# Other queues for q and gates, later weight requests, and values stored by row group in a layer of neighbourhood attention and retention

## The chip, the cores and the metric

The kernel runs on one core of one Trainium2 chip. Five engines work side by side, each with its own instruction queue: TensorE (PE; its weight loads are listed as PEld), VectorE (DVE), ScalarE (ACT), GpSimd (POOL) and SyncE (SP), which only issues DMAs. ScalarE issues DMAs too, between its computing instructions. A DMA that must wait (for a free buffer, or for data that is not there yet) holds every later instruction of the engine that issues it. The metric is the device time of one execution in microseconds (us), lower is better.

## What is computed

One layer for 2048 latent tokens (a grid of 32 rows by 64 columns) and 256 context tokens, width 1024, all in float32:

```python
h_lat = _rmsnorm(x, norm_g[i]) * (1.0 + scale) + shift          # adaLN from SiLU(c)
na_q, na_k, na_v, na_g, r_q, r_k, r_v, r_g = _split_proj(h_lat @ w_in)     # 8 parts of 512 columns
...
# group A: 8 heads of 64; each query reads an 8 x 16 window of the grid and all 256 context keys
s_loc = jnp.einsum('bhrqd,bhrkd->bhrqk', qr, kg, ...) * scale + bias[None]
p = jax.nn.softmax(jnp.concatenate([s_loc, s_ctx], axis=-1), axis=-1)
o = jnp.einsum('bhrqk,bhrkd->bhrqd', p_loc, vg) + jnp.einsum('bhrqc,bhcd->bhrqd', p_ctx, v_ctx)
y_na = _merge(o_na) * jax.nn.silu(na_g)
# group B: 4 heads of 128, retention in both directions, chunks of 128 tokens
y_ret = _head_rmsnorm(o_ret, ret_norm_g).astype(dt) * jax.nn.silu(r_g)
y_lat = jnp.concatenate([y_na, y_ret], axis=-1) @ w_out
x = x + gate * y_lat                                            # then one final RMSNorm
```

## The kernel before

The kernel keeps float32 accuracy by splitting an operand into a high and a low part (names `whi`, `wlo`, `hhi`, `hlo`) and adding three products. Results of the projection go to HBM (tensors `qS`, `kS`, `vS`, `gS` for group A; `rqS`, `rkS`, `rvS`, `ggS` for group B) and come back when they are needed. The stages, in time of the profiled execution:

- 0 to 156 us: norm, modulation and the k projection.
- 156 to 556 us: the first part of the projection: values of group A (`u_v`, 18 units of 256 tokens, two of them context, 166 to 280 us), gates, q of group A. Stores are issued by ScalarE here.
- 556 to 1082 us: neighbourhood attention, 128 tiles of 128 queries (8 rows by 16 columns): per head `h` four windows `i` of 8 rows, in each four tiles `j` of 16 columns. A tile's scores (`s_mm`) use the k tile of its head, `k2` (128 partitions: the high half of 64 dimensions on top of the low half) and the window's q tile, `q` (the same 64 rows in both halves of the partitions, two buffers). Softmax runs over VectorE (`s_min`), ScalarE (`s_exp`) and GpSimd (`s_norm`), transposes (`p_tr`) and the product with the values (`pv`) follow two and three tiles later. Values come as tiles `vt` of four grid rows, six buffers, with four slots by tile column: columns 0 to 23, 8 to 39, 24 to 55 and 40 to 63 (the table `CWIN`).
- Between the parts of a tile, `fill` runs steps of the rest of the projection (`fill_stream`: units of 8 steps for group B, four units to a weight block of 256 columns). It splits the next weights into high and low in pieces (`chop`), and `late_load` requests the block after.
- 1082 to 1430 us: retention and output projection.

All loads of the attention stage are on SyncE's queue, in the order in which the loop over tiles (at the end of `hybrid_kernel`'s attention part) calls them: `load_head` (k2 and the context values) once per head, at tile (1, 2) of the head before; `load_q` at the first tile of a window for the next window; `load_v` by group of four rows; `bias` for the three forms of position bias in a row of tiles; `load_gate` once per window; and, from `fill`, weights (`st`, line 173) and rotary tables (`rot`). A load of q is two DMAs of 64 rows, one for each half of the partitions; of k likewise; of a value group four, one for each tile column, each reading 4 grid rows of 24 or 32 positions.

Of the kernel before, what the change touches and what calls it, by code (L numbers as in the profile page):

```python
# [18 lines left out]
P = 128  # L19
# [55 lines left out]
        BN += _row[_c][0]  # L75
RTYPE = [0, 1, 1, 2]
CTYPE = [0, 1, 1, 2]


@with_exitstack  # L80
def hybrid_kernel(ctx: ExitStack, tc: tile.TileContext, a: dict, out: bass.AP):
# [3 lines left out]
    dram = ctx.enter_context(tc.tile_pool(name="dram", bufs=1, space=DRAM))  # L85
    qS = [dram.tile([4, P, 2, 512], F32, name=f"qS{t}") for t in range(4)]
    kS = [dram.tile([P, 2, LT], F32, name=f"kS{t}") for t in range(4)]
    vS = [dram.tile([LT, 4, P], F32, name=f"vS{t}") for t in range(2)]
    gS = [dram.tile([P, L], F32, name=f"gS{t}") for t in range(4)]
    rqS = [dram.tile([P, L], F32, name=f"rqS{r}") for r in range(RH)]  # L90
    rkS = [dram.tile([LT, 2 * P], F32, name=f"rkS{r}") for r in range(2)]
# [324 lines left out]
    def u_v(w, c0, tp):  # L416
        pm = yield from tokform(w, tp)
        vt = op.tile([P, 2, 2, 2, P], F32R, name="o")
        pv = pm.rearrange("p (t h e d) -> p t h e d", t=2, h=2, e=2)
        for e in range(2):  # L420
            hs, ls = slice(64 * e, 64 * e + 64), slice(64 - 64 * e, 128 - 64 * e)
            nc.scalar.copy(vt[:, :, :, e, hs], pv[:, :, :, e, :])
            nc.vector.tensor_tensor(vt[:, :, :, e, ls], pv[:, :, :, e, :], f(vt)[:, :, :, e, hs], ALU.subtract)
        store(vS[(c0 - 1024) // WG][tp * 256:(tp + 1) * 256].rearrange("(t p) h d -> p t (h d)", p=P),
              f(vt).rearrange("p t h e d -> p t (h e d)"))

    def put_tok(dstt, c0, tp, r, n=1):
        store(dstt[(c0 % 512) // WG][tp * 256:(tp + 1) * 256, :].rearrange("(t p) d -> p t d", p=P), r, n)
# [191 lines left out]
    def fill_stream(w):  # L620
        def units(kind, b):
            if kind is u_rq:
                return [(ct, b) for ct in range(2)]
            return [(2 * b + tp,) for tp in range(2)]

        def late_load(n):
            while chop:
                chop.pop(0)()
            if n == 0 and wseq:
                load_w()  # L630

        def next_c():
            w, parts = w_parts(*wcur.pop(0), n=4)
            chop.extend(parts)
            return w

        order = [(kind, *a_) for kind, c0 in fseq[:4] for b in range(2) for a_ in units(kind, b)]
        order += [(kind, *a_) for b in range(4) for kind, c0 in fseq[4:6] for a_ in units(kind, b)]
        order += [(kind, *a_) for kind, c0 in fseq[6:] for b in (2, 3) for a_ in units(kind, b)]
        at = [0]  # L640

        def needs(n):
            kind, *a_ = order[n] if n < len(order) else (None,)
            if kind is u_rk:
                return [("rot_k", a_[0])]
            if kind is u_rq and a_[0] == 0:
                return [("rot_c", a_[1]), ("rot_s", a_[1])]
            return []

        def steps(g):  # L650
            n = at[0]
            at[0] += 1
            is_rq = lambda k: k >= 0 and order[k][0] is u_rq
            if is_rq(n - 1):
                for e in needs(n)[1:]:
                    rot_load(*e)
            for m, v in enumerate(g):
                if m == 2:
                    for e in needs(n + 1)[:1 if is_rq(n) else 2]:
                        rot_load(*e)  # L660
                if chop:
                    chop.pop(0)()
                yield v

        for kind, c0 in fseq[:4]:
            wn = next_c()
            for n, args in enumerate(units(kind, 0) + units(kind, 1)):
                yield from steps(kind(w, c0, *args))
                late_load(n)
            w = wn  # L670
        (rk, ck), (rq, cq) = fseq[4:6]
        wn = next_c()
        for b in range(4):
            for n, args in enumerate(units(rk, b)):
                yield from steps(rk(w, ck, *args))
                late_load(n + b)
            if b == 3:
                w = next_c()
            for args in units(rq, b):
# [25 lines left out]

    def load_head(h):
        k2 = kp.tile([P, LT], F32R, name="k2")
        for hl in range(2):
            nc.sync.dma_start(f(k2)[64 * hl:64 * hl + 64, :], kS[h // 2][64 * (h % 2):64 * (h % 2) + 64, hl, :])
        vh = vS[h // 4][:, h % 4, :]  # L710
        vc = kp.tile([P, 2, P], F32R, name="vc")
        nc.sync.dma_start(f(vc), vh[L:, :].rearrange("(n p) d -> p n d", p=P))
        return dict(k2=k2, vh=vh, vc=vc, vt={}, q={})

    def load_q(hd, h, i):
        q = kp.tile([P, 2, 512], F32R, name="q", bufs=2)
        src = qS[h // 2][i, 64 * (h % 2):64 * (h % 2) + 64]
        for e in range(2):
            nc.sync.dma_start(f(q)[64 * e:64 * e + 64], src)
        hd["q"][i] = q  # L720

    def load_v(hd, gs):
        for g in gs:
            vt = kp.tile([P, 4, P], F32R, name="vt", bufs=6)
            src = hd["vh"][4 * g * GW:(4 * g + 4) * GW, :].rearrange("(r c) d -> r c d", c=GW)
            for j, (c0, cw) in enumerate(CWIN):
                nc.sync.dma_start(f(vt)[:4 * cw, j, :], src[:, c0:c0 + cw, :])
            hd["vt"][g] = vt

    def bias(h, rt, ct):  # L730
# [56 lines left out]
    def pv(t):  # L787
        h, i, j, kr0, kr, kc0, cw = dims(t)
        T, hd = tl_st[t], heads[h]
        pt, ng_ = T["pt"], T["ng"]  # L790
        if t % 2 == 0:
            tl_st["po"] = psc.tile([P, 2, 2, P], F32, name="po")
        po = tl_st["po"]
        cn = 4 * cw
        for g in range(ng_):
            nc.tensor.matmul(po[:, t % 2, :, :], hd["vt"][kr0 // 4 + g][:cn, j, :], pt[:cn, g, :, :], start=(g == 0), stop=False)  # L796
# [9 lines left out]
    def load_gate(t):  # L806
        h, i = dims(t)[:2]
        gts[t // 4] = ap_.tile([P, 512], F32, name="gt", bufs=2)
        nc.sync.dma_start(gts[t // 4][fin_(h)], gS[h // 2][fin_(h), i * 512:(i + 1) * 512])

    def combine(t):
        h, i, j = dims(t)[:3]
# [144 lines left out]
    for t in range(NT + 3):  # L957
        if t == 6:
            decay_exp(*dec)
        quota = (NF - held) * (t + 1) // (NT + 3) - done  # L960
        done += quota
        part = [quota // 3 + (quota % 3 > n) for n in range(3)]
        tick()
        if t < NT:
            s_mm(t)
        if 0 <= t - 1 < NT:
            s_norm(t - 1)
        fill(part[0])
        if t < NT:
            s_min(t)  # L970
        if 0 <= t - 2 < NT:
            p_tr(t - 2)
        if t < NT:
            s_exp(t)
        if 0 <= t - 2 < NT:
            p_lo(t - 2)
        fill(part[1])
        if 0 <= t - 3 < NT:
            pv(t - 3)
            if (t - 3) % 2 == 1:  # L980
# [12 lines left out]
        if i < 3 and j == 0:  # L993
            load_q(hd, h, i + 1)
        for g in {(0, 2): (3,), (0, 3): (4,), (1, 1): (5,), (1, 3): (6,), (2, 3): (7,)}.get((i, j), ()):
            load_v(hd, (g,))
        if h + 1 < NH:
            if i == 1 and j == 2:
                heads[h + 1] = load_head(h + 1)
            if i == 3:  # L1000
                nh = heads[h + 1]
                if j == 0:
                    load_q(nh, h + 1, 0)
                    bias(h + 1, 0, 0)
                    load_v(nh, (0,))
                if j == 2:
                    bias(h + 1, 0, 1)
                if j == 3:
                    bias(h + 1, 0, 2)
                    load_v(nh, (1, 2))  # L1010
    def load_y(lo, kind, t):
        half, o = t // 8, (t % 8) * P
        nc.sync.dma_start(f(lo), yS[half][4 * kind:4 * kind + 4, :, o:o + P].rearrange("k p t -> p k t"))
        return lo
# [331 lines left out]
```

## Time and profile before

| | us |
|---|---|
| median of 3 runs | 1429.25 (1426.46 to 1432.33) |
| the profiled execution, its own time | 1431.96 |
| its span, first to last instruction | 1430.0 |
| TensorE busy | 1351.1 (94%) |
| VectorE, ScalarE, GpSimd busy | 641.0, 531.0, 495.0 |
| mean granted clock of TensorE | 0.986 |
| moved by DMA | 264.14 MB, 185 GB/s over the span |

A row of windows gives a stretch of the span, each engine's busy time in it, the TensorE clock that was granted (1.00 is full), the mean busy share of the core's 16 DMA engines and the GB/s that they moved. A row of waits reads: who waited at which line, for whom, us in total, number of times, the longest. Rows of an instruction give its shortest, median and longest duration in ns; of a DMA that is the time of its issue, not of its transfer. SPq and ACTq are the queues on which SyncE and ScalarE issue.

### The profile page before, as it was taken

To read this page: it belongs to the slowest core of one execution; us is meant where nothing else is said; L and a number is where in the kernel's file an instruction comes from. 1 tells how busy PE (TensorE), PEld (TensorE's weight loads), DVE (VectorE), ACT (ScalarE), POOL (GpSimd) and SP (SyncE) were. 2 spreads that over 40 slices of the span, in tenths; PEclk is the share of its full clock that TensorE was granted. 3 is DMA by queue.
4 is the path that set the end of the run, shared out by engine and by line. 5 is a ranking of instruction groups with operands and counts; after the bars stand their busy time and mean duration, and the time that the engine had idled before them with its cause. 6 is when DMAs were issued, how large, how long until landed. Compare 5 with 4: busy or idle time off the path is not lost.

```text
span 1430.0 us, 22693 instructions
## 1 busy us (share of the span) xinstructions
PE 1351.1 (94%) x8380; PEld 1179.9 (83%) x8380; DVE 641.0 (45%) x1244; ACT 531.0 (37%) x1155; POOL 495.0 (35%) x499
## 2 busy tenths in 40 slices
PE   7989999999999999999899978798999989999997
PEld 2567899988887888998799877697999779888886
DVE  5786111100021222566666765476564544344445
ACT  5454212212212222655455433345563234333332
POOL 5442302202201221355354432235443144454442
PEclk9999999999999999999999998899999999999999
DMA  9444656223354677767758696867645998555433
GB/s 320 153 162 148 229 196 229 104 88 103 104 169 147 222 259 218 179 179 194 178 160 205 174 236 163 235 172 197 166 138 170 275 316 259 192 177 169 155 119 125
DMA packets 213072, 264.14 MB, mean 185 GB/s; under 512 B 14305, under 2 KB 160865, under 8 KB 211938
## 3 DMA queue, kind: packets, MB, share of 16 engines
q1 hardware_dynamic: 177282, 197.93, 48.1%
q10 hardware_dynamic: 35680, 64.76, 12.7%
q8 instruction: 67, 1.10, 0.3%
q14 instruction: 43, 0.35, 0.1%
HBM read 179.80 MB, written 82.84 MB: 184 GB/s over the span
## 4 chain that ended last, share of the span: by engine, by line
PE 73%; DMA 13%; DVE 7%; issue 2%; ACT 2%; POOL 2%; SPq 1%; ACTq 0%; DVEq 0%; POOLq 0%
PE mm L355 25%; PE mm L366 18%; PE mm L1190 10%; DMA q<-qS 5%; PE sS L748 4%; PE tr L775 2%; PE po L796 2%; DMA vt<-vS 2%; PE mm L915 2%; PE mm L299 2%; PE tr L777 1%; PE po L798 1%; DMA v<-rvS 1%; PE mm L1102 1%; PE mm L1101 1%
## 5 line engine op out<-in xcount | busy, mean ns | idle before, releaser
L355 PE MATMUL mm<-hhi,whi 128*128 128x512 f32 x640 | 260.0, 406 | 0.0
L355 PE MATMUL mm<-hlo,whi 128*128 128x512 f32 x640 | 254.0, 397 | 5.6 <-DVE hlo L268 2.2
L355 PE MATMUL mm<-hhi,wlo 128*128 128x512 f32 x640 | 253.8, 397 | 0.3 <-DVE wlo L336 0.3
L366 PE MATMUL mm<-whi,hhi 128*128 128x256 f32 x768 | 225.0, 293 | 0.0
L366 PE MATMUL mm<-wlo,hhi 128*128 128x256 f32 x768 | 217.3, 283 | 2.6 <-POOL wlo L336 2.6
L366 PE MATMUL mm<-whi,hlo 128*128 128x256 f32 x768 | 216.3, 282 | 0.0
L336 POOL TENSOR_TENSOR wlo<-st,whi 128x256 fp32r<-128x256 f32 (+1 forms) x97 | 112.3, 1175 | 251.1 <-ACT whi L334 250.8
L779 ACT CAST pt<-tr 128x640 fp32r<-128x640 f32 (+1 forms) x128 | 95.6, 747 | 217.9 <-PE tr L777 192.6
L785 DVE TENSOR_TENSOR pt<-tr,pt 128x640 fp32r<-128x640 f32 (+1 forms) x128 | 113.9, 890 | 105.2 <-ACT pt L779 104.6
L768 POOL TENSOR_SCALAR sp<-sp,stt 128x640 f32<-128x640 f32 (+2 forms) x128 | 103.7, 811 | 136.0 <-DVE stt L767 94.9
L366 PEld LDWEIGHTS mm<-wlo,hhi 128*128 128x128 f32 x768 | 145.4, 189 | 3.3 <-POOL wlo L336 3.2
L355 PEld LDWEIGHTS mm<-hlo,whi 128*128 128x128 f32 x640 | 121.0, 189 | 31.4 <-issue 3.2
L366 PEld LDWEIGHTS mm<-whi,hlo 128*128 128x128 f32 x768 | 145.7, 190 | 0.0
L366 PEld LDWEIGHTS mm<-whi,hhi 128*128 128x128 f32 x768 | 145.7, 190 | 0.0
L355 PEld LDWEIGHTS mm<-hhi,wlo 128*128 128x128 f32 x640 | 120.7, 189 | 29.5 <-DVE wlo L336 0.7
L355 PEld LDWEIGHTS mm<-hhi,whi 128*128 128x128 f32 x640 | 121.0, 189 | 28.5 <-issue 4.6
L757 DVE CUSTOM_DVE_ANT_0 sp<-sS,nb 128x640 f32<-128x640 f32 (+2 forms) x128 | 105.6, 825 | 53.4 <-PE sS L748 43.0
L748 PE MATMUL sS<-k,q 128*128 128x256 f32 (+3 forms) x512 | 101.7, 321 | 27.3 <-DMA q<-qS 21.8
L748 PEld LDWEIGHTS sS<-k,q 128*128 128x128 f32 x512 | 85.1, 192 | 36.5 <-issue 19.9
L762 ACT ACTIVATE sp<-sp,stt 128x640 f32<-128x640 f32 (+2 forms) x128 | 107.5, 839 | 20.1 <-DVE stt L757 19.8
L1190 PE MATMUL mm<-wor,y 128*128 128x512 f32 x384 | 95.6, 398 | 1.3 <-DVE xt L1199 1.2
L1190 PE MATMUL mm<-won,y 128*128 128x512 f32 x336 | 89.9, 406 | 0.0
(214 smaller groups left out, 2238.8 us busy)
## 6 DMA issues: line engine op xcount, KB each, us to landing
st<-in_w_in_dram SPq DMA_DIRECT2D x48, 512.0 KB
q<-qS SPq DMA_DIRECT2D x64, 256.0 KB
vS<-o ACTq DMA_DIRECT2D x18, 512.0 KB
k<-kS SPq DMA_DIRECT2D x16, 576.0 KB
kS<-o SPq DMA_DIRECT2D x16, 512.0 KB
woS<-g ACTq DMA_DIRECT2D x32, 256.0 KB
qS<-o ACTq DMA_DIRECT2D x16, 512.0 KB
vt<-vS SPq DMA_DIRECT2D x128, 64.0 KB
```

Of the source, the lines that this page charges most:

```text
L299: nc.tensor.matmul(aps[u][0:s.shape[2], :], s[:, 2 * j + k, :], w, start=(j == 0 and i == 0 and k == 0), stop=(j == 3 and i + 1 == len(ops ...
L336: eng.tensor_tensor(l, r, f(h), ALU.subtract)
L355: nc.tensor.matmul(pm[:, :n], ww[:, k, cs], h[:, k, :], start=(k == 0 and i == 0), stop=(k == KC - 1 and i == 2))
L366: nc.tensor.matmul(pm[:, t * WG:(t + 1) * WG], h[:, k, o:o + P], ww[:, k, :], start=(k == 0 and i == 0), stop=(k == KC - 1 and i == 2))
L748: nc.tensor.matmul(o, hd["q"][i][:, hl, j * P:(j + 1) * P], k, start=(hl == 0), stop=(hl == 1))
L757: nc.vector.tensor_tensor_reduce(T["sp"][:, :n], T["s"], nbz[big][:, o:o + n], -1.0, 3e38, ALU.add, ALU.min, T["st"][:, 0:1])
L762: nc.scalar.activation(sp[:, :n], sp[:, :n], AF.Exp, bias=st[:, 0:1], scale=-1.0, accum_out=st[:, 1:2])
L768: nc.gpsimd.tensor_scalar(sp[:, :n], sp[:, :n], st[:, 2:3], 0.0, ALU.mult, ALU.add)
L775: nc.tensor.transpose(tr[:cn, g, :], sp[:, T["lo"] + g * cn:T["lo"] + (g + 1) * cn], ident)
L779: nc.scalar.copy(pt[:, :ng_ + 2, 0, :], tr[:, :ng_ + 2, :])
L785: nc.vector.tensor_tensor(pt[:, :n, 1, :], tr[:, :n, :], f(pt)[:, :n, 0, :], ALU.subtract)
L1190: nc.tensor.matmul(pm, yy[:, k, :], ww[:, k, sl], start=(k == 0 and i == 0), stop=(k == 3 and i == 2))
```

## The change

Five things are edited.

1. `load_q` and `load_gate` are issued by ScalarE. `load_q` is one DMA instead of two: its source names the 64 rows twice, by a leading repeat of 2 with step 0.
2. `load_head` loads `k2` by one DMA whose source has the two halves as its leading dimension, then the 64 rows. It stays on SyncE's queue.
3. `late_load` requests the next weight block after the second unit of a block (`n == 1`), not after the first.
4. Latent values are stored in a new tensor `vB`, by group of four grid rows and tile column, in the form in which the attention reads them, so that columns that belong to two or three tile columns are stored that often. A unit of `u_v` issues eight stores (four tile columns, two row groups of 64 partitions) in place of one. `load_v` then loads a group by two DMAs, one of 128 partitions with two tile columns, one of 96 with the other two. Slots in a tile follow `VORD`.
5. Bias rows for the first window of the next head are loaded one tile later, the third of them at that head's first tile; so is the first value group of the next head.

```diff
+VORD = [1, 2, 0, 3]
...
-    vS = [dram.tile([LT, 4, P], F32, name=f"vS{t}") for t in range(2)]
+    vS = [dram.tile([LC, 4, P], F32, name=f"vS{t}") for t in range(2)]
+    vB = [dram.tile([P, 8, 4, 4 * P], F32, name=f"vB{t}") for t in range(2)]
...
-        store(vS[(c0 - 1024) // WG][tp * 256:(tp + 1) * 256].rearrange("(t p) h d -> p t (h d)", p=P),
-              f(vt).rearrange("p t h e d -> p t (h e d)"))
+        s, o = (c0 - 1024) // WG, f(vt).rearrange("p t h e d -> p t (h e d)")
+        if tp == 8:
+            store(vS[s].rearrange("(t p) h d -> p t (h d)", p=P), o)
+            return
+        for e, j in enumerate(VORD):
+            k0, cw = CWIN[j]
+            dst = vB[s][:4 * cw, tp, e, :].rearrange("(t r c) d -> r c t d", t=2, r=2)
+            for r in range(2):
+                store(dst[r], o[64 * r + k0:64 * r + k0 + cw])
...
-            if n == 0 and wseq:
+            if n == 1 and wseq:
                 load_w()
...
-                late_load(n + b)
+                late_load(n + 2 * b)
...
-        for hl in range(2):
-            nc.sync.dma_start(f(k2)[64 * hl:64 * hl + 64, :], kS[h // 2][64 * (h % 2):64 * (h % 2) + 64, hl, :])
+        nc.sync.dma_start(f(k2), kS[h // 2][64 * (h % 2):64 * (h % 2) + 64].rearrange("p e t -> e p t"))
...
         src = qS[h // 2][i, 64 * (h % 2):64 * (h % 2) + 64]
-        for e in range(2):
-            nc.sync.dma_start(f(q)[64 * e:64 * e + 64], src)
+        nc.scalar.dma_start(f(q).rearrange("p e t -> p (e t)"), src.rearrange("p e t -> p (e t)").unsqueeze(0).to_broadcast([2, 64, 1024]))
...
-            vt = kp.tile([P, 4, P], F32R, name="vt", bufs=6)
-            src = hd["vh"][4 * g * GW:(4 * g + 4) * GW, :].rearrange("(r c) d -> r c d", c=GW)
-            for j, (c0, cw) in enumerate(CWIN):
-                nc.sync.dma_start(f(vt)[:4 * cw, j, :], src[:, c0:c0 + cw, :])
+            vt, h = kp.tile([P, 4, P], F32R, name="vt", bufs=6), hd["h"]
+            for e, n in ((0, P), (2, 96)):
+                nc.sync.dma_start(f(vt)[:n, e:e + 2, :], vB[h // 4][:n, g, e:e + 2, (h % 4) * P:(h % 4 + 1) * P])
...
-        nc.sync.dma_start(gts[t // 4][fin_(h)], gS[h // 2][fin_(h), i * 512:(i + 1) * 512])
+        nc.scalar.dma_start(gts[t // 4][fin_(h)], gS[h // 2][fin_(h), i * 512:(i + 1) * 512])
...
                     load_q(nh, h + 1, 0)
+                if j == 1:
                     bias(h + 1, 0, 0)
                     load_v(nh, (0,))
-                if j == 2:
+                if j == 3:
                     bias(h + 1, 0, 1)
-                if j == 3:
-                    bias(h + 1, 0, 2)
                     load_v(nh, (1, 2))
+        if h > 0 and (i, j) == (0, 0):
+            bias(h, 0, 2)
```

Two places of the order in which instructions stand. SyncE's queue before, from the k load for a next head on (`kS`) to that head's first bias rows, q and gate (`nb`, `q`, `gt`) and a weight block (`st`):

```order
L709 DMA k_5975<-kS_62 64x2304 x2
L712 DMA vc<-vS_65 128x2x128
L727 DMA vt<-vS_65 96x1x128
L727 DMA vt<-vS_65 128x1x128 x2
L727 DMA vt<-vS_65 96x1x128
L732 DMA nb_3984<-in_rpb_t_dram 128x288
L719 DMA q<-qS_58 64x1024 x2
L732 DMA nb_3984<-in_rpb_t_dram 128x384
L809 DMA gt<-gS_68 64x512
L732 DMA nb_3984<-in_rpb_t_dram 128x288
L173 DMA st<-in_w_in_dram 128x4x256 x2
```

The same place of the changed kernel (its lines are numbered a little higher):

```order
L717 DMA k_6031<-kS_62 128x1x2304
L719 DMA vc<-vS_65 128x2x128
L732 DMA vt<-vB_67 128x2x128
L732 DMA vt<-vB_67 96x2x128
L737 DMA nb_4098<-in_rpb_t_dram 128x288
L737 DMA nb_4098<-in_rpb_t_dram 128x384
L737 DMA nb_4098<-in_rpb_t_dram 128x288
L732 DMA vt<-vB_67 128x2x128
L732 DMA vt<-vB_67 96x2x128
```

The k load is one DMA of 128 partitions, value groups are two, and q, gate and the weight block are gone from this place. ScalarE of the changed kernel, at the first tiles of the attention:

```order
L336 CAST whi<-st 128x256
L767 ACT_TABLE_LOAD
L767 ACTIVATE sp,stt<-sp,stt 128x544
L336 CAST whi<-st 128x256
L725 DMA q<-qS_57 128x1x1024
L336 CAST whi<-st 128x256
L767 ACTIVATE sp,stt<-sp,stt 128x640
L336 CAST whi<-st 128x256
L814 DMA gt<-gS_69 64x512
```

The q load stands behind the exponential of a window's first tile, the gate load behind that of its second. Before, ScalarE had neither.

More of the change, by code (lines that the diff above doesn't have):

```diff
@@ L707, in load_head @@
         k2 = kp.tile([P, LT], F32R, name="k2")
-        for hl in range(2):
-            nc.sync.dma_start(f(k2)[64 * hl:64 * hl + 64, :], kS[h // 2][64 * (h % 2):64 * (h % 2) + 64, hl, :])
-        vh = vS[h // 4][:, h % 4, :]
+        nc.sync.dma_start(f(k2), kS[h // 2][64 * (h % 2):64 * (h % 2) + 64].rearrange("p e t -> e p t"))
         vc = kp.tile([P, 2, P], F32R, name="vc")
-        nc.sync.dma_start(f(vc), vh[L:, :].rearrange("(n p) d -> p n d", p=P))
-        return dict(k2=k2, vh=vh, vc=vc, vt={}, q={})
+        nc.sync.dma_start(f(vc), vS[h // 4][:, h % 4, :].rearrange("(n p) d -> p n d", p=P))
+        return dict(k2=k2, h=h, vc=vc, vt={}, q={})
     def load_q(hd, h, i):
@@ L795, in pv @@
         for g in range(ng_):
-            nc.tensor.matmul(po[:, t % 2, :, :], hd["vt"][kr0 // 4 + g][:cn, j, :], pt[:cn, g, :, :], start=(g == 0), stop=False)
+            nc.tensor.matmul(po[:, t % 2, :, :], hd["vt"][kr0 // 4 + g][:cn, VORD.index(j), :], pt[:cn, g, :, :], start=(g == 0), stop=False)
         for g in range(2):
```

## The prediction

> **What bounds the kernel now.** I read the page first (busy time, the chain of waits), then the windows of the attention stage, then what TensorE and SyncE's queue wait for there.
>
> ```profile
> span 1430.0 us, 22693 instructions
> PE 1351.1 (94%) x8380; PEld 1179.9 (83%) x8380; DVE 641.0 (45%) x1244; ACT 531.0 (37%) x1155; POOL 495.0 (35%) x499
> PE 73%; DMA 13%; DVE 7%; issue 2%; ACT 2%; POOL 2%; SPq 1%; ACTq 0%; DVEq 0%; POOLq 0%
> ```
>
> TensorE is busy 94% of the span, so what is left to win is its idle 79 us and some lost clock. The windows (us, then busy time and instructions of PE, PEld, DVE, ACT, POOL, then granted clock, DMA share, GB/s) show where it is, and also how fast the DMA engines go with different loads in flight:
>
> ```profile
> 547.00:548.00 1.00, 1.00 (x6) 0.82 (x5) 0.00 (x0) 0.00 (x0) 0.00 (x0) 1.00 1.02 407
> 639.00:640.00 1.00, 1.00 (x11) 1.00 (x10) 1.00 (x3) 0.87 (x2) 0.80 (x1) 1.00 0.27 81
> 650.00:652.00 2.00, 2.00 (x19) 1.95 (x18) 0.99 (x3) 1.49 (x3) 1.68 (x2) 1.00 1.00 211
> 530.00:1058.00 528.00, 485.73 (x3456) 452.45 (x3455) 313.67 (x699) 252.11 (x526) 212.11 (x242) 0.97 0.71 189
> 556.00:1082.00 526.00, 483.73 (x3547) 455.54 (x3546) 324.79 (x725) 261.70 (x546) 218.86 (x247) 0.97 0.69 183
> 166.50:216.30 49.80, 49.80 (x420) 49.80 (x421) 6.81 (x16) 5.97 (x16) 4.60 (x2) 1.00 0.64 233
> ```
>
> The attention stage, 556 to 1082 us, has 526 - 483.73 = 42.3 us of idle TensorE, at a mean clock of 0.97. Its 128 tiles take 4.11 us each, so a window of four tiles takes 16.4 us and a head 65.8. What TensorE waits for there, and what SyncE's queue waits for from 156 to 1120 us (total, times, longest):
>
> ```profile
> PE sS L748 <- DMA q<-qS: 21.8, 7, 6.6
> PE po L796 <- DMA vt<-vS: 7.0, 2, 3.9
> PE tr L775 <- DVE pt L785: 4.7, 5, 1.9
> SPq L173 <- POOL wlo L336: 186.0, 22, 38.7
> SPq L732 <- DVE stt L757: 46.0, 19, 5.2
> ```
>
> TensorE waits for q and v tiles. They are late because they stand on SyncE's one queue behind weight requests (L173) that wait for GpSimd and bias loads (L732) that wait for VectorE. The change attacks exactly this: q and gate loads leave that queue, weights are asked for later, bias rows one or two tiles later.
>
> **What the change adds: narrow loads.** Every load names how its bytes are cut. The v loads of before read 4 grid rows of 24 or 32 positions each, so the source's outermost count is 4. SyncE's timeline (start, duration, number) and the two windows above show what that does:
>
> ```profile
> 634.99 3.68 SPq L727 DMA_DIRECT2D vt<-vS  x6
> 638.77 1.32 SPq L719 DMA_DIRECT2D q<-qS  x2
> 645.23 1.66 SPq L709 DMA_DIRECT2D k<-kS  x2
> ```
>
> By 638.67 all six v loads are issued, and a q load is issued behind them. Yet from 639 to 640 the DMA share is 0.27: 4.3 of 16 engines work, at 81 / 4.3 = 19 GB/s each, and twelve stand still although work is queued. The issue rate can't be the limit, since no v load is issued in that time. The k loads of before (64 rows, outermost count 64) give a share of 1.00 from 650 to 652. So a load whose source has an outermost count of 4 runs on four engines, always the same four while several are queued (otherwise the share would rise).
>
> The changed q load reads its 64 rows twice by a leading repeat of 2; the changed k load puts the two halves first, again 2. Neither is in the trace; the nearest row is the four-row v load, and by it they run on **two** engines. The other end is 16 engines, as the 64-row loads have. I take two: it is the same property, one step on. The v loads, by contrast, get an outermost count of 128 or 96 and leave the four engines for all.
>
> [...] No run here shows a count of two.
>
> **The sum, on the two shared engines.** What has to pass them:
>
> ```profile
> q<-qS SPq DMA_DIRECT2D x64, 256.0 KB
> k<-kS SPq DMA_DIRECT2D x16, 576.0 KB
> q1 hardware_dynamic: 177282, 197.93, 48.1%
> L719 SPq DMA_DIRECT2D q<-qS x64: 444/540/1966, 539.7 to 1045.8; - x64
> L709 SPq DMA_DIRECT2D k<-kS x16: 480/592/1285, 530.5 to 978.7; - x16
> ```
>
> - q: 64 x 256 KB = 16.8 MB (as 32 loads of 512 KB), k: 16 x 576 KB = 9.4 MB (as 8 of 1152 KB). Half on each engine: 8.39 and 4.72 MB, 13.1 MB.
> - Speed of one busy engine: at best 407 / (1.02 x 16) = 24.9 GB/s. So q 337 us, k 190 us, 527 us in all: a q load takes 10.5 us, a k load 23.7.
> - The rest of the traffic still takes its sixteenth of each engine. From 530 to 1058 us 528 x 189 GB/s = 99.8 MB moved; less q and k 73.6 MB, 4.6 MB per engine. At 24.9 GB/s that is 185 us; at SyncE's queue mean, 197.93 MB / (0.481 x 16 x 1430 us) = 18.0 GB/s, 256 us. Its packets are small ones in part, so I take the middle, 220.
> - Sum 712 to 783 us, 747 taken. Before, these loads and that traffic had 528 us. The two engines become the bound of the stage.
>
> The first k load is issued at 530.5; 530.5 + 747 = 1278 us is when the last q lands, if the two engines never stand still. In the trace of before the last window's first score (288 local keys, an edge tile) runs here, with 20.2 us to the stage's end at 1082:
>
> ```profile
> 1061.83 0.42 PE L748 MATMUL sS<-k,q 128*128 128x288 f32 x2
> ```
>
> So the stage ends near 1298, **216 us later**. Do the two engines stand still? A q tile is requested after its window's predecessor's first tile, 12.3 us before it is wanted, and the load alone takes 10.5, with the other queue's packets between up to twice that. Without a k load in flight the demand per window is 10.5 + 220/32 = 17.4 us against 16.4 us of work, already full; with one it is 23.7 us more. I add nothing, and leave 40 us for it in the range. If k loads keep the pace of 650 to 652, 211/16 = 13.2 GB/s per engine, the 4.72 MB take 358 us instead of 190: 168 us more, the upper bound.
>
> Requests that stand behind a k load on SyncE's queue (the next group of v, the bias, the weights) have their share on the two engines behind it too, so TensorE will also wait for v and weights; that time is in the sum, since the engines work meanwhile.
>
> **The edits with small terms.**
>
> ```profile
> 193.58 0.37 ACT L422 CAST o<-mm 128x256 fp32r<-128x256 f32 x1 [4.44 <-PE mm L366]
> 195.31 0.37 ACTq L147 DMA_DIRECT2D vS<-o  x1
> 199.26 0.37 ACT L422 CAST o<-mm 128x256 fp32r<-128x256 f32 x1 [4.44 <-PE mm L366]
> L809 SPq DMA_DIRECT2D gt<-gS x32: 444/451/1675, 563.3 to 1061.0; - x32
> L727 SPq DMA_DIRECT2D vt<-vS x256: 504/616/1790, 543.5 to 1059.2; - x128
> ```
>
> *Values stored in eight pieces.* A unit of the value projection takes 5.68 us (193.58 to 199.26). ScalarE copies for 1.73 us and issues one store of 0.37; now eight, 3.0 us by that row, 3.6 by the gate loads (0.451), 4.9 by the v loads (0.616). 1.73 + 3.6 = 5.3 fits; 6.7 would cost 1.0 x 16 units = 16 us. The stores write 112 of every 64 columns, 896 KB a unit instead of 512; 393 KB / 5.68 us = 69 GB/s on top of 233 raises the share of 0.64 to 0.83. But each piece comes from 24 or 32 partitions, and the k loads of 64 got half of 407 GB/s. Were a piece of 32 bound to a quarter, and the pieces to go one by one, a unit's stores would take 8 x 1.29 = 10.3 us: 74 us more over 16 units. Pieces of both row groups are in flight together, so I take 5 us of 0 to 74.
>
> *q and gates on ScalarE's queue.* 64 issues of 0.45 us, 29 us on an engine with 264 us free in the stage; they come after a tile's exponential, when their buffers are long free, so no wait joins them. *Weights one unit later*: a unit is about 13 us (3.2 tiles) of the 53 between requests; they keep 40. *Bias later*: each still has three or more tiles, 12 us. These cost nothing and would win the 28.8 us of q and v waits, if the loads themselves were not slower; that win has no place in the sum.
>
> Total: 1431.96 + 216 + 5 = **1653 us**, in the profiled execution's terms; it lies 2.7 above the median of 1429.25, which is nothing beside this.
>
> **The rivals.**
>
> *Wide after all (faster).* The loads are spread over 16 engines whatever the source's outer count. Then the queue change does its work: the q and v waits, 28.8 us, go, or at most the 42.3 idle us. 1390 to 1405, say 1400. For it: nothing in the trace shows a count of 2. Against it: the 0.27. Chance 0.05.
>
> *Four engines and hidden (faster).* The least spread seen is four. 26.2 MB / 4 / 24.9 GB/s = 263 us, plus 220 is 483 us in 528: it fits, q comes from a queue of its own, and most of the q wait goes: 1412. Against it: nothing explains four from a count of two. Chance 0.04.
>
> *ScalarE held by the issue (slower still).* A q load puts a share on two engines that is eight times as long as before; if the issuing engine stands until it has room, ScalarE can't do the exponentials for 10.5 us in each of 32 windows: 336 us, 1770. Against it: SyncE issued six v loads in 3.68 us although they then took longer than that to move. Chance 0.1.
>
> **How the numbers follow.** Forecast (two engines bound the stage) 0.81, with its own range 1600 to 1760; ScalarE held 0.1; wide 0.05; four engines 0.04. The range is 1585 (712 us of demand gives 1618, less some traffic that finds room before 530 or after 1058) to 1800 (most of the 168 us for slow k loads, or ScalarE held). A measurement here tells half a per cent from no change. Faster is wide, four engines: 0.08 with 0.01 of them falling to no change; slower 0.91, that is 0.81 + 0.1.
>
> **What would show it.** Right: TensorE's wait for q at the scores grows from 21.8 to over 120 us, and waits for k, v or weights with it; the stage is some 750 us long; its DMA share falls to about half (the same 96 MB in more time, near 130 GB/s); short windows with only q or k in flight have a share near 0.13; ScalarE's q issues last under 1 us. The value projection (166 to 280) stays within 10 us. Wrong: a share near 1 while q loads run, or a stage of 526 us or less. Issues of q of 10 us would mean the third rival; a wait of TensorE or ScalarE for the value stores, the 74 us.

## The result, and the profile after

The changed kernel takes 1736.01 us (median, 1733.41 to 1737.76), beside 1427.86 for the kernel before on the same chip: 1.2154 times as long, 95% interval 1.2116 to 1.2192. It is 308 us slower; the forecast was 1653, 221 slower. The sign, the place and the mechanism came as predicted, and 83 us are missing from the sum; the time lies inside the range of 1585 to 1800.

The page of the changed kernel, its span and busy times:

```profile
span 1734.8 us, 22654 instructions
PE 1410.3 (81%) x8380; PEld 1232.8 (71%) x8380; DVE 641.7 (37%) x1244; ACT 530.2 (31%) x1155; POOL 492.9 (28%) x499
```

TensorE has the same 8380 matmuls, now 81% of the span instead of 94%. What TensorE waits for from 556 to 1400 us, and then windows of the same kernel:

```profile
PE sS L753 <- DMA q<-qS: 213.3, 27, 26.9
PE tr L780 <- DVE pt L790: 29.7, 4, 18.5
PE mm L357 <- DVE o L387: 17.4, 1, 17.4
PE po L801 <- DMA vt<-vB: 2.1, 1, 2.1
```

```profile
612.00:620.00 8.00, 0.00 (x0) 0.00 (x0) 0.00 (x0) 0.00 (x0) 0.00 (x0) 0.65 0.13 53
641.00:644.00 3.00, 3.00 (x22) 2.91 (x22) 1.77 (x5) 1.43 (x4) 0.03 (x1) 0.88 0.03 3
556.00:1390.00 834.00, 558.82 (x3680) 523.86 (x3679) 329.76 (x731) 263.96 (x551) 219.78 (x251) 0.82 0.38 121
```

TensorE's wait for q went from 21.8 to 213.3 us, in 27 of 32 windows. From 612 to 620 no computing engine works, a q load and a k load are both in flight, and the DMA share is 0.13: 2.1 of 16 engines work, and two engines that move 53 GB/s move 26.5 each. That is the narrow load as predicted, and both loads share one pair of engines, or the share would be 0.25. The second row is the surprise: from 641 to 644 the share is 0.03. In the middle of the stage that these two engines are said to bound, they stand nearly still.

Where the time lies shows in the first and last start of the scores' matmuls, before and after:

```profile
L748 PE MATMUL sS<-k,q x512: 274/291/660, 561.4 to 1072.9; 128*128 128x256 f32 x86, 128*128 128x384 f32 x44, 128*128 128x512 f32 x21, 128*128 128x288 f32 x20
```

```profile
L753 PE MATMUL sS<-k,q x512: 274/333/660, 597.8 to 1373.9; 128*128 128x256 f32 x86, 128*128 128x384 f32 x44, 128*128 128x512 f32 x21, 128*128 128x288 f32 x20
```

The first score comes 36.4 us later, the scores take 776.1 us in place of 511.5 (264.6 more), and from the last score to the end it is 360.9 against 357.1. 36.4 + 264.6 + 3.8 is the 304.8 by which the span grew. The windows of the scores alone, before and after:

```profile
561.40:1072.90 511.50, 469.23 (x3446) 442.12 (x3445) 319.33 (x714) 257.34 (x538) 216.04 (x244) 0.97 0.70 185
597.80:1373.90 776.10, 518.35 (x3446) 488.49 (x3444) 320.67 (x714) 257.10 (x538) 215.09 (x244) 0.82 0.39 121
```

Of the 264.6 us, 215.5 are idle time of TensorE (42.3 before, 257.8 after); its wait for q alone grew by 191.5. The other 49.1 are busy time: the same matmuls take 518.35 us instead of 469.23, at a granted clock of 0.82 instead of 0.97. From 612 to 620, with TensorE idle, the clock is 0.65.

### The profile page after: what moved, and what is told of

The parts are those of the page before. It is cut to its first block, busy times and chain, and to the rows that moved or that the text cites. A ratio compares the mean times of both kernels' runs of the same rounds, so it can differ in the third digit from the quotient of the medians.

```text
span 1734.8 us, 22654 instructions
## 1 busy us (share of the span) xinstructions
PE 1410.3 (81%) x8380; PEld 1232.8 (71%) x8380; DVE 641.7 (37%) x1244; ACT 530.2 (31%) x1155; POOL 492.9 (28%) x499
## 5 line engine op out<-in xcount | busy, mean ns | idle before, releaser
L753 PE MATMUL sS<-k,q 128*128 128x256 f32 (+3 forms) x512 | 113.1, 348 | 223.2 <-DMA q<-qS 213.3
L357 PE MATMUL mm<-hhi,whi 128*128 128x512 f32 x640 | 264.3, 413 | 19.3 <-DVE o L387 17.4
L753 PEld LDWEIGHTS sS<-k,q 128*128 128x128 f32 x512 | 94.2, 213 | 234.4 <-issue 224.2
L368 PE MATMUL mm<-whi,hhi 128*128 128x256 f32 x768 | 234.7, 306 | 6.0 <-ACT whi L336 6.0
L368 PE MATMUL mm<-wlo,hhi 128*128 128x256 f32 x768 | 225.6, 294 | 3.9 <-POOL wlo L338 3.9
L368 PE MATMUL mm<-whi,hlo 128*128 128x256 f32 x768 | 224.8, 293 | 0.0
L368 PEld LDWEIGHTS mm<-whi,hhi 128*128 128x128 f32 x768 | 155.0, 202 | 6.2 <-ACT whi L336 6.2
L368 PEld LDWEIGHTS mm<-wlo,hhi 128*128 128x128 f32 x768 | 154.2, 201 | 4.6 <-POOL wlo L338 4.6
L368 PEld LDWEIGHTS mm<-whi,hlo 128*128 128x128 f32 x768 | 154.9, 202 | 0.0
L780 PE MATMUL tr<-ident,sp 128*128 128x128 f32 (+1 forms) x448 | 80.5, 303 | 29.9 <-DVE pt L790 29.7
```

Source lines behind the costliest of these rows:

```text
L357: nc.tensor.matmul(pm[:, :n], ww[:, k, cs], h[:, k, :], start=(k == 0 and i == 0), stop=(k == KC - 1 and i == 2))
L368: nc.tensor.matmul(pm[:, t * WG:(t + 1) * WG], h[:, k, o:o + P], ww[:, k, :], start=(k == 0 and i == 0), stop=(k == KC - 1 and i == 2))
L753: nc.tensor.matmul(o, hd["q"][i][:, hl, j * P:(j + 1) * P], k, start=(hl == 0), stop=(hl == 1))
L780: nc.tensor.transpose(tr[:cn, g, :], sp[:, T["lo"] + g * cn:T["lo"] + (g + 1) * cn], ident)
```

## The experiments

Each run is a whole kernel with all its outputs. A ratio is to the kernel before on the same chip, with its 95% interval. "Scores" is the time from the first score's matmul to the last, read from the row shown above (before 511.5, after 776.1 us).

### One load made wide, the other left narrow

The first run takes the changed kernel and splits q into the two 64-row loads of before, still on ScalarE's queue; k stays one narrow load:

```diff
-        nc.scalar.dma_start(f(q).rearrange("p e t -> p (e t)"), src.rearrange("p e t -> p (e t)").unsqueeze(0).to_broadcast([2, 64, 1024]))
+        for e in range(2):
+            nc.scalar.dma_start(f(q)[64 * e:64 * e + 64], src)
```

> The changed kernel with the q load as two DMAs of 64 rows again, still on ScalarE's queue; the k load stays one DMA with an outermost count of 2. Theory (two engines carry q and k, and the stage is paced by them): without q the pair has k, 4.72 MB at 26.5 GB/s (53 GB/s from 612 to 620 us on two engines), 178 us, and 4.7 MB of the rest, some 210 us, 390 us in all against 528: no bound. Left are requests that stand behind a k load on SyncE's queue, 0 to 40 us, and the slower value projection, 17 us: 1445 to 1485 us, TensorE's wait for q under 40 us. Rival one (ScalarE's queue brings q late, whatever its form): stays above 1650 with a wait for q near 200 us. Rival two (the values' new form is the cost): stays above 1650 too, with waits for v.

Measured: 1538.28 us, 1.0778 (1.0754 to 1.0803), scores 585.7 us. Slower than the 1445 to 1485 expected, and far under the 1650 of both rivals. TensorE hardly waits for q any more (8.0 us); SyncE's queue waits for k loads:

```profile
SPq L733 <- DMA k<-kS: 69.6, 4, 21.1
SPq L175 <- DMA k<-kS: 22.6, 1, 22.6
SPq L405 <- DMA k<-kS: 16.3, 1, 16.3
```

The rows are v loads (L733), weights (L175) and rotary tables (L405), held up to 22.6 us at a time until a k load has landed.

The second run does the opposite: k in two loads as before, q as in the change.

```diff
-        nc.sync.dma_start(f(k2), kS[h // 2][64 * (h % 2):64 * (h % 2) + 64].rearrange("p e t -> e p t"))
+        for hl in range(2):
+            nc.sync.dma_start(f(k2)[64 * hl:64 * hl + 64, :], kS[h // 2][64 * (h % 2):64 * (h % 2) + 64, hl, :])
```

> The changed kernel with the k load as two DMAs of 64 rows again; the q load stays narrow. Theory: the pair has q, 326 us, and the rest, 210, 536 us against 528: just a bound. But q is asked for one window ahead only, and in the last head, where no k load runs, a q load took 14 us and the next was asked for about 6 us after it landed: 20 us per window against 16.4. So 32 x 3.6 = 115 us over the stage, and 17 for the values: 1540 to 1600 us. If only the amount on the two engines counts and not the loop of request and landing: 1445 to 1470. Rivals one and two as in the run of q: above 1650.

Measured: 1614.36 us, 1.1311 (1.1282 to 1.1339), scores 680.9 us. That is 14 us over the 1540 to 1600 expected; the 1445 to 1470 of a cost by the amount alone is out. TensorE waits 131.6 us for q, in 27 windows. A window takes 21.3 us, more than the 17.4 that the prediction had as its demand.

### Both wide, and the old values with them

The third run makes both replacements and keeps the rest of the change.

> The changed kernel with both loads as pairs of 64-row DMAs; queues, weight requests and the values' form stay as changed. Theory: nothing is narrow any more; q no longer waits behind weights, so TensorE's wait for q (21.8 us before) falls under 8 us, less 15 to 30 us in the stage, against 17 us more in the value projection: 1405 to 1435 us. Rival one (ScalarE's queue): above 1650. Rival two (values): above 1650.

Measured: 1417.6 us, 0.9911 (0.9879 to 0.9943), scores 479.1 us. As expected: without the two narrow loads nothing of the loss is left. Against this run the narrow k alone costs 585.7 - 479.1 = 106.6 us of scores, the narrow q alone 201.8, both 297.0. The two add up to 308.4, nearly the sum; they hide little of one another.

The fourth run is the third with the values stored and loaded in the form of before, so that only queues and request times differ from the kernel before.

> As the run with both loads in pairs, and the values stored and loaded as in the kernel before (one store a unit, four loads a group on four engines). What is left of the change: q and gates on ScalarE's queue, weights one unit later, bias and the first value group later. Theory: the value projection is as short as before (17 us less than in the changed kernel), q waits are gone, waits for v stay (7 us) or grow a little: 1395 to 1415 us. If the later bias and value loads cost more than the queues win: 1425 or more.

Measured: 1457.22 us, 1.021 (1.0189 to 1.0231), scores 527.4 us. The theory missed, in sign; the other branch (1425 or more) came. The edits that the prediction let cost nothing lose 2.1% beside the old values, and the new form of the values is what makes the third run faster.

### The values alone

The kernel before with the new tensors, eight stores and two loads; q, k, gates, weights and bias as before. Its loads, the stores being those of the change:

```diff
-            for j, (c0, cw) in enumerate(CWIN):
-                nc.sync.dma_start(f(vt)[:4 * cw, j, :], src[:, c0:c0 + cw, :])
+            for e, n in ((0, P), (2, 96)):
+                nc.sync.dma_start(f(vt)[:n, e:e + 2, :], vB[h // 4][:n, g, e:e + 2, (h % 4) * P:(h % 4 + 1) * P])
```

> The kernel before with the new form of the values alone (eight stores per unit, two loads per group); q, k, gates, weights and bias as before, all on SyncE's queue. The runs so far give the new form a gain of 39.6 us in company with the new queues (1457.2 to 1417.6). If that gain is the values' own, it comes here too: 1385 to 1395. If the new queues made the old value loads dear and the new form only pays that back, the values by themselves save part of the 28.8 us of q and v waits and cost some 14 in the value projection: 1415 to 1432.

Measured: 1407.39 us, 0.9843 (0.9818 to 0.9867), scores 467.6 us. Between the two expectations: the values' own gain is 22 us, and it is there without any other edit. They take 43.9 us from the scores (511.5 to 467.6) and lose 17.0 before them (first score at 578.4 instead of 561.4). The window of the scores, and TensorE's wait for q in this run and in the fourth (q on ScalarE's queue, old values):

```profile
578.40:1046.00 467.60, 456.12 (x3446) 433.07 (x3445) 319.61 (x714) 257.12 (x538) 215.69 (x244) 1.00 0.73 201
PE sS L755 <- DMA q<-qS: 3.1, 2, 1.9
PE sS L748 <- DMA q<-qS: 10.7, 3, 5.8
```

Of the 43.9 us, 30.8 are idle time of TensorE (42.3 before, 11.5 here) and 13.1 busy time, at a granted clock of 1.00 instead of 0.97. With q on SyncE's queue as before, the wait for q falls from 21.8 to 3.1 us by fewer and wider v loads alone; in the fourth run, with another queue but the old v loads, 10.7 us of it stay.

### The spills

The 17 us lost before the scores lie in the value projection. ScalarE's timeline in the changed kernel (start, duration, number of stores) has two long entries, and from 160 to 300 us ScalarE waits for stores to free its tiles:

```profile
173.93 12.02 ACTq L149 DMA_DIRECT2D vB<-o  x8
200.56 3.50 ACTq L149 DMA_DIRECT2D vB<-o  x8
240.91 10.03 ACTq L149 DMA_DIRECT2D vB<-o  x8
```

```profile
ACT o L424 <- DMA vB<-o: 79.8, 15, 12.6
```

A normal unit issues its eight stores in 3.5 us, which fits; the first unit of each half takes 10 to 12. At these two places SyncE stores the 16 pieces of 512 KB of the embedded input (`hS`), the spills. The run moves these behind the value units, on top of the run with both loads wide:

```diff
-                spill_step()
+                if j >= 4:
+                    spill_step()
```

> The run with two q loads and two k loads (1417.6 us) with one thing moved: the sixteen spill stores of the embedded input on SyncE's queue start with the fifth group of projection units, behind the value units. Theory (ScalarE's eight value stores of the first unit of each half are held 10 to 12 us because these large stores are in flight): the holds go, the first gate copy comes near 289 us in place of 302, and the time is 1404 (1398 to 1410). Rival (the eight pieces themselves cost the 14 us, whatever else is in flight): 1414 to 1421.

Measured: 1401.11 us, 0.9805 (0.9782 to 0.9829), as expected. The same entries, and the group of waits, are:

```profile
171.60 4.95 ACTq L149 DMA_DIRECT2D vB<-o  x8
205.73 3.50 ACTq L149 DMA_DIRECT2D vB<-o  x8
229.53 4.17 ACTq L149 DMA_DIRECT2D vB<-o  x8
ACT o L424 <- DMA vB<-o: 57.8, 13, 5.5
```

The long holds are gone, and the first score comes at 560.5 in place of 577.5. The eight pieces cost little by themselves; in company with the spills they cost 17 us. No run moves the spills in the kernel before with its old stores, so whether that kernel would gain by the move too is not known.

The same edit on the kernel before with the values alone:

> The kernel before with the new form of the values alone (1407.4 us) and the spill stores moved behind the value units, as in the run that gained 16.5 us by it (1417.6 to 1401.1). The gain should be the same, as the value projection is the same: 1393 (1388 to 1398), less than both kernels. If the spills are needed earlier than the gate units let them through, or if the gain there came from elsewhere: 1402 to 1409.

Measured: 1393.65 us, 0.977 (0.9732 to 0.9807), as expected. It beats both kernels, 2.3% under the one before.

### Is it the queue of q and gates?

The run with both loads wide and the spills later, with q and gate loads issued by SyncE again; weights and bias stay late.

> The run with two q loads, two k loads and the spills later (1401.1 us) with q and gate loads back on SyncE's queue; weights and bias stay asked for later. The values alone are 10 us faster than the whole change with wide loads (1407.4 against 1417.6). If the move to ScalarE's queue costs these 10 us (an issue there that waits holds the exponentials), they come back here: 1389 to 1395. If the later weights and bias cost them, nothing comes back: 1399 to 1405.

Measured: 1396.82 us, 0.9779 (0.9751 to 0.9806), beside 0.9805 (0.9782 to 0.9829) with q and gates on ScalarE's queue. It fell between the two expectations and the intervals overlap. In one profile of each the scores take 468.5 us against 479.5, which points to the queue, but the first score comes later there (565.9 against 560.5), and by the times it is not settled whether the queue or the late requests make these edits lose.

### Do the two engines stand still between requests?

The last windows of the changed kernel, in its chain of waits (start, length, what):

```profile
1284.57 14.23 DMA q<-qS
1304.54 13.85 DMA q<-qS
1324.62 14.14 DMA q<-qS
1345.32 15.77 DMA q<-qS
```

About every 20 us the chain goes through a load for 14, from its request to its landing; then come some 6 until the next request, which stands on ScalarE behind the exponential of the next window's first tile. With two buffers it could not come much earlier, since the buffer that it fills is read until the window before is done. To break this loop, the run with a wide k and a narrow q gets a third q buffer and asks for q two windows ahead (one gate buffer less pays for it, the gate comes two tiles later):

```diff
-        q = kp.tile([P, 2, 512], F32R, name="q", bufs=2)
+        q = kp.tile([P, 2, 512], F32R, name="q", bufs=3)
...
-        if i < 3 and j == 0:
-            load_q(hd, h, i + 1)
+        if i < 2 and j == 0:
+            load_q(hd, h, i + 2)
+        if i >= 2 and j == 0 and h + 1 < NH:
+            load_q(heads[h + 1], h + 1, i - 2)
```

> The narrow q load stays and the k load is wide, as in the run with two k loads (1614.4 us, 680.9 us from the first score to the last, 21.3 per window); new is that a q load is requested two windows ahead (a third q buffer, paid for with one gate buffer less, the gate loaded two tiles later). Theory (the two engines stand still between one request and the next: 14 us from request to landing, then some 6 until the next request): with the next load always queued the packets bind, q 326 us by its packets in the trace of the change, the rest 212, k's sixteenth 24, 562 in all or 17.6 per window; the stage shrinks by about 119 us, and the time is 1495 (1460 to 1535). Rival (the engines' amount was already the bound, or the queues are held until earlier DMAs land, which a deeper q queue makes no better): it stays within 25 us of 1614.

Measured: 1561.62 us, 1.0928 (1.0897 to 1.0958), scores 625.0 us. Between theory (1495) and rival (within 25 us of 1614). The loop was real: 53 us came back, and TensorE's list of waits no longer names q. But the rest did not come. TensorE now waits for transposes that ScalarE makes room for late, and ScalarE's timeline (start, duration, instruction, and in brackets its idle time before and what ended it) shows why:

```profile
PE tr L781 <- DVE pt L791: 81.7, 21, 10.7
```

```profile
690.80 0.19 ACT L768 ACTIVATION_READ_ACCUMULATOR sp<-sp,stt 128x1 f32 x1
704.30 0.47 ACTq L149 DMA_DIRECT2D yS<-y  x1
704.86 0.80 ACT L785 CAST pt<-tr 128x768 fp32r<-128x768 f32 x1 [13.87 <-DMA q<-qS]
```

From 691 to 704.3 ScalarE stands before a store of y, and what releases it is the landing of a q load, with which that store has nothing to do. Its y was ready, since the gate load issued at 690.43 had waited for the GpSimd multiplication that writes it. The program's order on ScalarE, with what each instruction waits for, at this place:

```
555 L815 DMA gt<-gS_69 64x512 [waits DMAHW1_49,Pool_49]
556 L149 DMA yS_85<-y_5237 64x512 [waits DMAHW2_49]
557 L785 CAST pt<-tr 128x6x128 [waits DVE_49,PE_49]
```

The only wait of the store is one of eight DMA semaphores (DMAHW0 to 7), which in this program's listing serve the 991 loads and stores of both queues. By the program's order and by the profile the transfer before it on this one was a q load. So here a q load in flight held a store that came to the same semaphore next, and ScalarE, which issues it, stood 13.87 us. In the changed kernel SyncE's v loads (L732) wait that way too, 78.3 us in all, for q loads that they don't need:

```profile
SPq L732 <- PE po L801: 177.9, 23, 28.9
SPq L732 <- DMA q<-qS: 78.3, 11, 14.3
SPq L737 <- DMA k<-kS: 44.8, 3, 18.8
```

The same kernel with q issued by GpSimd, so that in its listing no q load has one of these eight semaphores:

> As the run with a wide k load and a narrow q load two windows ahead (1561.6 us, 628 us from the first score to the last, TensorE no longer waiting for q but ScalarE standing before its own issues), with q issued from GpSimd's queue. Theory (those 628 less the 562 of packets are ScalarE held until earlier transfers have landed): the stage is 562 to 580, the time 1495 to 1515. Rival (other loads crawl on the two engines beside q's packets, whoever issues): 1545 to 1570.

Measured: 1495.03 us, 1.047 (1.0445 to 1.0496), scores 554.4 us; 66.6 us less than from ScalarE's queue. The time is at the lower end of the theory's, and the scores take less than the 562 us that packets on one pair were to take. It is not clean proof of the theory, as the next two runs show: GpSimd's queue changes one thing more.

### The narrow loads on GpSimd's queue

The run with a wide q and a narrow k, with k issued by GpSimd, away from v, bias and weights:

> q as two loads, the narrow k load as in the change (1538.3 us with k on SyncE's queue), but k issued from GpSimd's queue. Theory (the 106 us of the narrow k load are loads of v, bias and weights that stand behind it on SyncE's queue): they are free of it, and the time is near the run with both loads wide, 1425 to 1445, with a share of 0.13 gone from short windows only where other work is in flight. Rival (the amount on the two engines is the cost, whoever issues it): 1515 to 1545.

Measured: 1518.82 us, 1.0633 (1.06 to 1.0666), scores 562.8 us. The rival's range holds: of the 120.7 us between a narrow k (1538.28) and both wide (1417.6) only 19.5 came back. A k load there lands 34.8 us after its issue (median). SyncE's v loads now wait for bias and v loads, wide ones, to land, 24.6 us at the longest:

```profile
SPq L733 <- DMA nb<-in_rpb_t_dram: 53.2, 12, 24.6
SPq L733 <- DMA vt<-vB: 20.3, 10, 4.2
```

What holds these wide loads is not shown, since no row gives a single engine.

And the whole change, with both narrow loads on GpSimd's queue and q two windows ahead:

> The whole change with its narrow q and k loads, but both issued from GpSimd's queue, and q two windows ahead (third q buffer, one gate buffer less). No issue on ScalarE's or SyncE's queue can wait for such a load any more. Theory (the amount on two engines is the floor, 326 for q, 178 for k, 212 for the rest by packet times, and 747 by the prediction's sum): first score to last takes 716 to 750 in place of 776, the time is 1675 to 1710. Rival (the amount is not the bound, only the standing queues are): the stage comes under 640, the time under 1600. Third (GpSimd is held by these loads, and normalises late): 1740 and more.

Measured: 1537.63 us, 1.0787 (1.0718 to 1.0855), scores 580.6 us. That is far under the floor of 716, and the theory as it was put falls; the rival's numbers (stage under 640, time under 1600) came. Two windows of it, the first with two q loads and a k load in flight, the second a few us later:

```profile
563.00:571.00 8.00, 5.29 (x23) 3.94 (x21) 0.00 (x0) 0.00 (x0) 0.00 (x0) 1.00 0.40 155
574.00:579.00 5.00, 0.00 (x0) 0.00 (x0) 0.00 (x0) 0.00 (x0) 0.00 (x0) 0.50 0.13 51
```

The second has a share of 0.13, two engines, as before; but the first, three loads in flight with a few other packets, has 0.40, 6.4 engines. So the narrow loads from GpSimd's queue had more than one pair between them, which the expectation had not counted on. What was the floor of one pair is no floor then, and the run doesn't test it. Nor does it tell how much of its gain over the change (198 us) is due to more engines, how much to free queues, and how much to the earlier request.

## Why the prediction was right, and where its sum fell short

**What held.** The reading of the 0.27 share of v loads, that "a load whose source has an outermost count of 4 runs on four engines", taken one step on to a count of 2, is shown by the 0.13 of the narrow loads. That q and k, from ScalarE's and SyncE's queues, share one pair is shown by the same row. That this is the cause is shown by the run with both loads wide: it alone turns 1.2154 into 0.9911. Most of the signs came too: the wait for q (213.3 us, over 120), the DMA share of the stage (0.38, 121 GB/s), q issues under 1 us. One did not: TensorE was to wait for k, v or weights as well, and waited 2.1 us for v. The first two rivals (wide after all; four engines) fall with the 0.13. Of the third, ScalarE held by the issue of q, the form that was predicted is false:

```profile
L725 ACTq DMA_DIRECT2D q<-qS x32: 527/537/640, 558.1 to 1345.3; - x32
L717 SPq DMA_DIRECT2D k<-kS x8: 510/511/661, 548.5 to 1223.1; - x8
L732 SPq DMA_DIRECT2D vt<-vB x128: 315/457/8111, 556.8 to 1352.8; - x128
```

No q issue is longer than 640 ns. What took long is the issue of other loads: single v loads up to 8.1 us on SyncE's queue (at 570.05, with the q load issued at 558.1 in flight), and one gate load 5.4 us on ScalarE's, at 1229.83, soon after the q load of 1227.1 and the k load of 1223.1.

**The amount on the two engines: right, slightly high.** At the measured 26.5 GB/s per engine, q takes 8.39 / 0.0265 = 317 us and k 178, 495 where the prediction had 527. The rest, an estimate by the long window: 834 us x 121 GB/s = 100.9 MB, less 26.2 MB, a sixteenth of it 4.67 MB; at 18.0 to 26.5 GB/s 176 to 259 us, where the prediction had 220. Together 671 to 754, with 747 predicted; the middle is 713. The upper bound, k at 13.2 GB/s, did not occur: the narrow k has 26.5.

**The step that failed is "Do the two engines stand still?", answered with "I add nothing, and leave 40 us for it in the range".** The first k load is issued at 548.5 and the last q has landed at 1345.3 + 15.8 = 1361, 812 us later. Less 713 of work, the two engines stood still for some 100 us by this estimate (58 to 141 by the ends of the rest). Two reasons were found. The first is shown by a run: the next q load is asked for only after the one before has landed and the first tile behind it is done, so in a window without a k load the pair goes idle after the landing (the loop of 14 + 6 us, and the share of 0.03 from 641 to 644; asking earlier gave 53 us back). The prediction had both parts of this loop (12.3 us from request to need in a window of 16.4, and 10.5 to twice that for the load) but did not add them: 20 us is more than the 17.4 that it took as a window's demand. The second is in part argued: of requests behind a k load the prediction says that "that time is in the sum, since the engines work meanwhile", and it overlooked that slow loads also hold DMAs that don't need them, on both issuing engines (78.3 us of SyncE's v loads for q, 26.6 of ScalarE before the stage); while these are held, they queue nothing new for the pair. The 66.6 us by which q from GpSimd's queue is faster fit that, but how much of them more engines gave is not shown. That the time still fell inside the range is in part luck: its upper part was kept for slow k loads or a ScalarE held by the issue of q, and neither came.

The sum also has no term for the clock. TensorE's busy time in the scores grew by 49.1 us at 0.82 instead of 0.97. Some of it may lie in the shadow of loads in flight, some may lengthen the 6 us of the loop; no run separates these.

In terms of the time: the prediction had +216 for the stage and +5 for the values. Measured are +264.6 for the scores, 49 more, and 36.4 before the first score. Of these 36.4, 20.3 are the narrow loads (first score at 597.8, with both wide 577.5), ahead of the stage, on ScalarE, where it was predicted that "no wait joins" (waits of ScalarE from 500 to 620 us):

```profile
ACT o L386 <- DMA q<-qS: 26.6, 1, 26.6
```

A copy of the q projection stood 26.6 us behind a store that stands on ScalarE's queue behind the first narrow q load. By the program's order that store waits for the semaphore that this q load raises, as in the run with q two windows ahead, and the first score comes after it.

**The values' stores: +5 of 0 to 74 predicted, 17 measured.** The issue time was well estimated (3.6 against 3.5 us a unit) and the pieces of 24 or 32 partitions are no limit by themselves (with the spills later the first score came at 560.5, beside 561.4 in the kernel before). (The 74 took all eight pieces as 32 wide; with four of them 24 wide, the same sum gives some 53.) The 17 us came from the spill stores in flight at the same time, and went when these were moved. The value projection was to stay within 10 us; it did not.

**The edits "at nothing" were not free.** Moving q and gates to ScalarE, asking later for weights and bias: with the old values these cost 2.1%. With the new ones and wide loads the kernel takes 1417.6 us against 1407.39 for the values alone, on another chip but at ratios of 0.9911 and 0.9843. The prediction expected them to win up to 28.8 us. Which of them loses was not separated. And the v loads, of which it only said that they "leave the four engines for all", are the part with the gain, 43.9 us of scores: 30.8 of the 42.3 us of TensorE's idle time, and 13.1 at a higher clock.

**Open** stays how much of the narrow k's 120.7 us is other loads landing late beside it and how much held queues: GpSimd's queue gave back 19.5, but from that queue the share of narrow loads was another (0.40 for three).

## What to carry to other kernels

In these runs the share of the DMA engines followed a load's leading dimension, 1.00 at 64 rows, 0.27 at 4 and 0.13 at 2: read from a short window of the trace whether a load in flight alone has the share that its size deserves, before its bytes are counted against the whole chip's rate. A saving of one DMA issue (0.54 us, the median of a q load's) is nothing beside a load that is eight times as narrow, and with narrow k loads on GpSimd's queue SyncE's v loads still waited 53.2 us for wide bias loads to land. When a sum says that a resource is nearly full, ask what keeps it fed: with one request ahead and two buffers it stood still for about an eighth of the time, by the estimate above, and a store that waited on a semaphore shared with a q load held ScalarE for 13.87 us, though neither needed that load.

## What the hardware did that was not expected

- Narrow loads from ScalarE's and SyncE's queues had two engines between them (a DMA share of 0.13 with a q and a k load in flight together), but from GpSimd's queue three narrow loads together had 0.40. The same bytes in the same shape took 1537.63 us in place of 1736.01 there, with q asked for earlier.
- An engine of the pair was no slower with narrow loads: 26.5 GB/s each, against the 24.9 of all sixteen together. The 13.2 GB/s per engine that the 64-row k loads showed is not a property of the k data.
- The issue of a small DMA took up to 8.1 us (median 0.457) in the changed kernel. With k on GpSimd's queue a v load on SyncE's still took 8.782 us; whether a k load was in flight then is not shown. A first unit's eight value stores took 12.02 us in place of 3.50 while 512 KB stores ran from another queue.

```profile
L733 SPq DMA_DIRECT2D vt<-vB x128: 320/450/8782, 552.1 to 1141.8; - x128
```
